# Transposes of a bank queued and issued one by one behind wide products, and the first activation sums of the MLP one piece later

## The chip, the cores and the metric

The kernel runs on one core of a Trainium2 chip. Time is device microseconds of one launch. TensorE (PE in the profile, with its weight loads as PEld) does matrix products and transposes, VectorE (DVE) and ScalarE (ACT) elementwise work, GpSimd (POOL) small work and some DMAs, SyncE (SP) issues most DMAs. Each engine works through its own list of instructions in order; semaphores hold an instruction until what it needs is there.

## The reference, cut to what matters

Two layers on 256 tokens of width 2048: an attention mixer (MLA) with an MLP, then a Mamba-2 mixer (SSM) with an MLP. Every mixer and MLP reads a normalised residual stream and adds to it.

```python
def squared_relu_mlp(h, w_in, w_out):          # 2048 -> 8192 -> 2048
    u = jax.nn.relu(h @ w_in)
    return (u * u) @ w_out

def reference(...):
    for i in range(DEPTH):                     # DEPTH = 2
        h = rms_norm(x, mix_norm_g[i])
        mix = mla_mixer(h, ...) if i % 2 == 0 else ssm_mixer(h, ...)
        x = x + mix
        h = rms_norm(x, mlp_norm_g[i])
        x = x + squared_relu_mlp(h, mlp_w_in[i], mlp_w_out[i])
    return x
```

The result must have float32 quality, and nearly all of the time goes into products of activations and weights.

## The kernel before, in words

**Products in halves.** Weights come from memory in pieces of 128 x 1024 floats (a "unit", tile `raw` or `rx`). ScalarE copies each to a rounded high half `wh` (line 102), VectorE subtracts that from the original to get the low half `wl` (line 103). [...] Activations are held in the same way, as a high and a low tile. A product is then three matrix products into one PSUM bank: high x high, low x high, high x low. These are the **wide products**, 128 x 128 weights of TensorE (an activation tile) against 512 columns: lines 339, 340 and 343 in `block`, and 616, 617 and 618 in `products` inside the MLP. 9216 of them, with 192 of 384 columns, fill most of TensorE's list. A unit of the MLP gives 6 or 12 of them.

**Transposes.** A product wants its activations with the contracted dimension on the partitions, so each result (128 tokens x 512 columns) is transposed before it can be used. `transposed` (line 316) takes a PSUM bank, issues four 128 x 128 transposes into its four quarters, and hands the bank to `split_out` (line 298): ScalarE copies it to the high tile (299), VectorE subtracts to the low tile (300). A transpose is a product with the identity `ident`, in one of two forms: as float32 (line 324), or as float32r words (line 322), for which GpSimd has first copied the source by DMA into a tile `tr`. A bank has three words and a float one, four of words, or four floats. The bank comes from the pools `sm` and `yp`, two banks each, or `sm` alone.

**Who calls it.** `finalize` at the ends of mixers and of the first MLP (both token tiles of one quarter of the width), `latent` in the MLA (queries `cq`, compressed keys and values `ckv`), `z_block` in the SSM, and `hidden` in the MLP, for each of the 32 activation blocks of an MLP. They are called with a delay: `later(n, fn)` runs `fn` n + 1 ticks on, and a tick follows each group of products; in the MLP, `turn` puts them in a list `due` with a time in microseconds, and `move` advances that clock by 1.36 or 2.72 per unit and runs what is due. The four transposes of a bank (or eight, where two calls are due together) thus stand in one row between two units.

**The order of the lists.** TensorE's list is in the order in which the code is written (`manual_schedule`). The lists of the other engines are ordered by a scheduler, by its own idea of when operands will be ready; so moving transposes also moves instructions on VectorE and ScalarE.

**The MLP's start.** The MLP forms sums of quarters of the weights and of the activations, so that seven products do the work of eight. The sums of weights are VectorE's line 183 (a weight tile plus another, both loaded by SyncE's DMAs at line 85). The sums of activations are `steps` from `combinations`: `one` (two whole tiles and more by line 528, a difference by line 538, a split to `sN`), `two` (more of these) and `three`. The first MLP product blocks need no sums (pieces `c`, eight units of 2.72 us by the clock in `move`); during them the sums are run, `when(5, steps[0])` and `when(10, steps[1])`: at the first piece whose end reaches 5 and 10 us, so behind the second and the fourth.

**Buffers.** Raw weights have 6 buffers, `wh` and `wl` 4 each. A load waits on SyncE until VectorE has read the tile that held its buffer.

Of the kernel before, what the change touches and what calls it, by code (L numbers as in the profile page):

```python
# [28 lines left out]
P = 128  # L29
# [29 lines left out]
class Unit:  # L59
# [3 lines left out]
    def __init__(self, key, nk, n, loads, make):  # L63
        self.key, self.nk, self.n, self.loads, self.make = key, nk, n, loads, make
# [150 lines left out]
class Trunk:  # L215
    def __init__(self, tc, ctx, d, out):
        self.tc, self.nc, self.d, self.out = tc, tc.nc, d, out
        nc = self.nc
        pool = lambda name, bufs, **kw: ctx.enter_context(tc.tile_pool(name=name, bufs=bufs, **kw))
        self.c = pool("const", 1)  # L220
        self.st = pool("stat", 24)
        self.res = pool("res", 1)
        self.xtp = pool("xt", 8)
        self.k4 = pool("k4", 8)
        self.s2 = pool("s2", 7)
        self.gb = pool("gb", 2)
        self.wp = {"raw": pool("raw", 6), "wh": pool("wh", 4), "wl": pool("wl", 4)}
        self.acc = pool("acc", 4, space=PSUM)
        self.sm = pool("sm", 2, space=PSUM)
        self.yp = pool("yp", 2, space=PSUM)  # L230
        self.queue, self.pump = [], None
        self.nsm = 0
        self.uid = 0

# [19 lines left out]
    def drain(self):  # L254
        while self.queue:
            self.tick()

    def stat(self, n):
        return self.st.tile([P, 16], F32, tag="st", name=self.name("st"))[:, :n]
# [54 lines left out]
        self.transposed(src, h[:, :, sl], lo[:, :, sl], wide)  # L314

    def transposed(self, src, h, lo, wide=True):
        b = self.bank(wide)
        src, words, n = src if isinstance(src, tuple) else (src, None, 0)
        for j in range(4):
            v = slice(j * P, (j + 1) * P)  # L320
            if j < n:
                self.nc.tensor.transpose(b.bitcast(F32R)[:, v], words[:, v], self.ident_r)  # L322
            else:
                self.nc.tensor.transpose(b[:, v], src[:, v], self.ident)  # L324
        self.split_out(h, lo, b.rearrange("p (k n) -> p k n", k=4))


    def block(self, keys, lhs, n=512, accs=None, first=True, last=True, mid=None):
        nc = self.nc
        if accs is None:  # L330
            accs = [self.acc_tile() for _ in range(2)]
        kt = 0
        for ik, key in enumerate(keys):
            for nk, wh, wl, end in self.flow.piece(key):
                en = last and ik == len(keys) - 1 and end
                for q in range(nk):
                    for t in range(2):
                        ah, al = lhs(kt + q, t)
                        nc.tensor.matmul(accs[t][:, :n], ah, wh[:, q, :], start=first and kt + q == 0, stop=False)  # L339
                        nc.tensor.matmul(accs[t][:, :n], al, wh[:, q, :], start=False, stop=False)  # L340
                for q in range(nk):
                    for t in range(2):
                        nc.tensor.matmul(accs[t][:, :n], lhs(kt + q, t)[0], wl[:, q, :], start=False, stop=en and q == nk - 1)  # L343
                kt += nk
                if mid and not end:
                    mid()
            self.tick()
        return accs
# [210 lines left out]
    def mlp_body(self, mp, layer, gain):  # L559
# [25 lines left out]
        S, steps = self.combinations(mp, xa)  # L585
        S["M1"], S["N4"], S["M2"] = xa[0, 0], xa[1, 1], xa[1, 0]
        out, bank, v, count = {}, {}, {}, {}
# [3 lines left out]
        def when(us, fn):  # L591
            due.append((at[0] + us, fn))
# [16 lines left out]
        def products(accs, key, lhs, kt, first, last):  # L609
            u, (h, lo) = self.flow.next(key)  # L610
            for q in range(2):
                k = 2 * kt + q
                wh, wl = h[:, q * 512:(q + 1) * 512], lo[:, q * 512:(q + 1) * 512]
                for t, b in enumerate(accs):
                    ah, al = lhs(k, t)
                    nc.tensor.matmul(b, ah, wh, start=first and q == 0, stop=False)  # L616
                    nc.tensor.matmul(b, ah, wl, start=False, stop=False)  # L617
                    nc.tensor.matmul(b, al, wh, start=False, stop=last and q == 1)  # L618

        sub = lambda o, a, b: nc.vector.tensor_tensor(o, a, b, ALU.subtract)  # L620
        plus = lambda o, a, b: nc.vector.tensor_tensor(o, a, b, ALU.add)
# [29 lines left out]

        tokens = plan()
        inside = False
        when(5, steps[0])
        when(10, steps[1])
        for tok in tokens:
            key = (tok[0], layer) + tok[1:]
            if tok[0] == "s":
                _, p, name, d = tok
# [3 lines left out]
                if count.setdefault(name, 0) % 4 == 0:  # L663
                    pool = self.sm if name == "N7" else self.acc
                    bank[name] = pool.tile([P, 512], F32, tag=pool.name, name=self.name("st"))
                count[name] += 1
                products([bank[name]], key, lambda k, t: [x[:, k] for x in S[name]], d,
                         count[name] % 4 == 1, count[name] % 4 == 0)
                if count[name] % 4 == 0:
                    after(name, p)  # L670
                move(1.36)
            elif tok[0] == "c":
                _, p, j, o = tok
                if o == 0:
                    out["c"] = pair_of_banks(self.yp if j else self.acc)
                products(out["c"], key, lhs_x, o, o == 0, o == 7)
                if o == 7:
                    for t in range(2):
                        turn(relu(out["c"][t], t), p, j, t, TR[4])
                    if j:  # L680
                        when(3, steps[2])
                if o % 2:
                    self.tick()
                move(2.72)
            else:
                _, p, nb, o = tok
                if o == 0:
                    out[nb] = pair_of_banks(self.yp)
                products(out[nb], key, lhs_u(p), o, o == 0, o == 3)
                if o == 3:  # L690
                    self.add_residual(nb, out.pop(nb))
                move(2.72)
# [915 lines left out]
```

## Time and profile before

| what | value |
|---|---|
| runs | 2287.46 us median of 3 (2285.67 to 2288.2) |
| profiled execution, first to last instruction | 2284.5 us |
| transposes of line 322 (words) | 229 into `sm`, 20 into `yp` |
| transposes of line 324 (floats) | 167 into `sm`, 16 into `yp` |
| weight splits, lines 102 and 103 | 986 each |
| loads of `wraw` and `wrx` from the page's DMA list | 512 KB each, 4.0 to 7.8 us to landing |

How to read the views that follow. A timeline row has the start in us, the length in us, engine, line, operation, out<-in, shape and count; rows of the same kind that follow each other are merged. A group row has busy us and the mean of one instruction in ns, then idle time before it. TensorE's products overlap, so their lengths say little; from one start to the next is what one costs. A weight load (PEld) begins as a rule when the product ahead of it starts.

### The profile page before, as it was taken

How to read it: one execution, taken by the hardware profiler on the slowest of the kernel's cores; microseconds unless marked ns; L12 is line 12 of the kernel's file. 1: busy time of each engine (PE TensorE's matmuls, PEld its weight loads, DVE VectorE, ACT ScalarE, POOL GpSimd, SP SyncE). 2: the span in 40 equal slices, each digit the busy share in tenths (PEclk: the TensorE clock that was granted, in tenths of full speed). 3: DMA queues.
4: the chain of work that ended last, by engine and by line, in shares of the span. 5: the costliest groups of instructions: out<-in, count | busy, mean ns of one | idle time of the engine just before them, and what ended most of it. 6: DMA issues, size and time to landing. Idle time of an engine off the chain costs nothing.

```text
span 2284.5 us, 30768 instructions
## 1 busy us (share of the span) xinstructions
PE 2278.1 (100%) x10929; PEld 1889.6 (83%) x10929; DVE 1915.9 (84%) x2318; ACT 1390.1 (61%) x1947; POOL 275.5 (12%) x315
## 2 busy tenths in 40 slices
PE   9999999999999999999999999999999999999999
PEld 7898888888888888888888888888888888888887
DVE  7786698999898897687899688676989889989985
ACT  7775576566666666564666555545666666666663
POOL 1440000000000000100133213121000000000000
PEclk9999999999999999999999999999999999999999
DMA  8545678888888878667888787767688888888874
GB/s 315 173 153 159 211 230 267 259 255 270 264 255 259 267 232 271 227 208 241 277 280 278 245 275 264 229 222 229 204 265 248 259 270 253 260 275 247 267 232 160
DMA packets 167706, 557.16 MB, mean 244 GB/s; under 512 B 19040, under 2 KB 28192, under 8 KB 166528
## 3 DMA queue, kind: packets, MB, share of 16 engines
q1 hardware_dynamic: 151264, 502.44, 66.2%
q0 software_dynamic: 13888, 48.49, 10.0%
q10 hardware_dynamic: 2400, 4.27, 0.5%
q8 instruction: 86, 1.41, 0.3%
q14 instruction: 68, 0.56, 0.1%
HBM read 529.65 MB, written 6.41 MB: 235 GB/s over the span
## 4 chain that ended last, share of the span: by engine, by line
PE 96%; DVE 1%; DMA 1%; ACT 1%; issue 1%; POOL 0%; SPq 0%; ACTq 0%; DVEq 0%
PE acc L339 13%; PE acc L340 13%; PE acc L343 13%; PE yp L618 9%; PE yp L617 9%; PE yp L616 9%; PE st L617 7%; PE st L618 7%; PE st L616 7%; DMA wraw<-mi 1%; PE sm L324 1%; DVE wl L103 1%; PE y L1309 1%; PE sm L322 1%; PE acc L616 1%; PE acc L618 1%
## 5 line engine op out<-in xcount | busy, mean ns | idle before, releaser
L102 ACT ACTIVATE wh<-wraw 128x1024 fp32r<-128x1024 f32 (+1 forms) x818 | 856.2, 1053 | 570.4 <-PE acc L340 268.9
L103 DVE TENSOR_TENSOR wl<-wraw,wh 128x1024 fp32r<-128x1024 f32 (+1 forms) x818 | 985.5, 1221 | 240.6 <-ACT wh L102 216.6
L616 PE MATMUL yp<-wh,k 128*128 128x512 f32 x896 | 349.2, 390 | 0.0
L618 PE MATMUL yp<-wh,k 128*128 128x512 f32 x896 | 348.8, 389 | 0.0
L617 PE MATMUL yp<-wl,k 128*128 128x512 f32 x896 | 348.6, 389 | 0.0
L339 PE MATMUL acc<-wh,xt 128*128 128x512 f32 x704 | 279.7, 397 | 0.4 <-ACT wh L102 0.4
L340 PE MATMUL acc<-wh,xt 128*128 128x512 f32 x704 | 274.9, 390 | 0.1
L102 ACT ACTIVATE wh<-wrx 128x1024 fp32r<-128x1024 f32 x168 | 177.8, 1058 | 153.4 <-PE yp L618 101.7
L103 DVE TENSOR_TENSOR wl<-wrx,wh 128x1024 fp32r<-128x1024 f32 x168 | 204.3, 1221 | 36.6 <-ACT wh L102 35.6
L618 PEld LDWEIGHTS yp<-wh,k 128*128 128x128 f32 x896 | 168.2, 188 | 35.1
L617 PEld LDWEIGHTS yp<-wl,k 128*128 128x128 f32 x896 | 168.2, 188 | 34.9
L616 PEld LDWEIGHTS yp<-wh,k 128*128 128x128 f32 x896 | 168.2, 188 | 34.8
L339 PE MATMUL acc<-wh,k 128*128 128x512 f32 x496 | 196.5, 396 | 0.0
L340 PE MATMUL acc<-wh,k 128*128 128x512 f32 x496 | 193.3, 390 | 0.0
L343 PE MATMUL acc<-wl,xt 128*128 128x512 f32 x704 | 188.3, 389 | 0.0
L616 PE MATMUL st<-wh,xt 128*128 128x512 f32 x448 | 177.7, 397 | 0.0
L618 PE MATMUL st<-wh,xt 128*128 128x512 f32 x448 | 174.9, 390 | 0.0
L617 PE MATMUL st<-wl,xt 128*128 128x512 f32 x448 | 174.7, 390 | 0.0
L339 PEld LDWEIGHTS acc<-wh,xt 128*128 128x128 f32 x704 | 132.7, 188 | 29.4 <-ACT wh L102 1.6
L340 PEld LDWEIGHTS acc<-wh,xt 128*128 128x128 f32 x704 | 132.5, 188 | 28.5 <-issue 1.2
L343 PEld LDWEIGHTS acc<-wl,xt 128*128 128x128 f32 x704 | 132.1, 188 | 27.7
L199 POOL DMA_DIRECT2D wrx<-mi x56 | 49.2, 878 | 720.6 <-DVE wl L103 524.5
(318 smaller groups left out, 3527.0 us busy)
## 6 DMA issues: line engine op xcount, KB each, us to landing
wraw<-mi SPq DMA_DIRECT2D x256, 512.0 KB, 5.5
wraw<-mo SPq DMA_DIRECT2D x256, 512.0 KB, 5.6
wraw<-si SPq DMA_DIRECT2D x160, 512.0 KB, 5.2
wraw<-so SPq DMA_DIRECT2D x64, 512.0 KB, 5.2
wrx<-mi SPq DMA_DIRECT2D x56, 512.0 KB, 5.4
wrx<-mi POOLq DMA_DIRECT2D x56, 512.0 KB, 7.8
wraw<-wo SPq DMA_DIRECT2D x32, 512.0 KB, 4.0
taps<-xD SPq DMA_DIRECT2D x16, 768.0 KB, 8.4
```

The source lines that it names most:

```text
L102: self.last = nc.scalar.activation(h[:, v], raw[:, v], AF.Copy)
L103: self.last_lo = nc.vector.tensor_tensor(lo[:, v], raw[:, v], h[:, v].bitcast(F32), ALU.subtract)
L199: nc.gpsimd.dma_start(st["b11"].tile, quarter(d, 1, 0), accum_op=ALU.add)
L322: self.nc.tensor.transpose(b.bitcast(F32R)[:, v], words[:, v], self.ident_r)
L324: self.nc.tensor.transpose(b[:, v], src[:, v], self.ident)
L339: nc.tensor.matmul(accs[t][:, :n], ah, wh[:, q, :], start=first and kt + q == 0, stop=False)
L340: nc.tensor.matmul(accs[t][:, :n], al, wh[:, q, :], start=False, stop=False)
L343: nc.tensor.matmul(accs[t][:, :n], lhs(kt + q, t)[0], wl[:, q, :], start=False, stop=en and q == nk - 1)
L616: nc.tensor.matmul(b, ah, wh, start=first and q == 0, stop=False)
L617: nc.tensor.matmul(b, ah, wl, start=False, stop=False)
L618: nc.tensor.matmul(b, al, wh, start=False, stop=last and q == 1)
L1309: nc.tensor.matmul(y[t][c, o], part(t)[:, c], xg[g][t][:, o], start=True, stop=True)
```

## The change

`transposed` no longer issues its four transposes. It puts four functions in a list `drops`; each, when called, issues one transpose (the first also takes the bank, the fourth also issues `split_out`). `drip` runs the first function of the list. Behind every wide product, `block` and `products` call `drip` once. `flush` empties the list at the very end. In the MLP the times of `one` and `two` go from 5 and 10 to 8 and 12, so they run behind the third and the fifth piece.

```diff
+        self.drops = []
...
+    def drip(self):
+        if self.drops:
+            self.drops.pop(0)()
+
+    def flush(self):
+        while self.drops:
+            self.drip()
...
     def transposed(self, src, h, lo, wide=True):
-        b = self.bank(wide)
         src, words, n = src if isinstance(src, tuple) else (src, None, 0)
-        for j in range(4):
-            v = slice(j * P, (j + 1) * P)
+        bank = []
+
+        def one(j):
+            if not bank:
+                bank.append(self.bank(wide))
+            b, v = bank[0], slice(j * P, (j + 1) * P)
             if j < n:
                 self.nc.tensor.transpose(b.bitcast(F32R)[:, v], words[:, v], self.ident_r)
             else:
                 self.nc.tensor.transpose(b[:, v], src[:, v], self.ident)
-        self.split_out(h, lo, b.rearrange("p (k n) -> p k n", k=4))
+            if j == 3:
+                self.split_out(h, lo, b.rearrange("p (k n) -> p k n", k=4))
+
+        for j in range(4):
+            self.drops.append(lambda j=j: one(j))
...
                         nc.tensor.matmul(accs[t][:, :n], ah, wh[:, q, :], start=first and kt + q == 0, stop=False)
+                        self.drip()
                         nc.tensor.matmul(accs[t][:, :n], al, wh[:, q, :], start=False, stop=False)
+                        self.drip()
...
                         nc.tensor.matmul(accs[t][:, :n], lhs(kt + q, t)[0], wl[:, q, :], start=False, stop=en and q == nk - 1)
+                        self.drip()
...
                     nc.tensor.matmul(b, ah, wh, start=first and q == 0, stop=False)
+                    self.drip()
                     nc.tensor.matmul(b, ah, wl, start=False, stop=False)
+                    self.drip()
                     nc.tensor.matmul(b, al, wh, start=False, stop=last and q == 1)
+                    self.drip()
...
-        when(5, steps[0])
-        when(10, steps[1])
+        when(8, steps[0])
+        when(12, steps[1])
```

In TensorE's list the transposes before stand in 48 rows of three word transposes and a float one, 16 rows of four float ones, 15 rows of seven and one, and 7 rows of eight float ones: 249 and 183. After, each of the 432 has a wide product ahead of it and one behind it. In the lists below the number behind a tile's name is its place in the program, and the lines of the changed kernel are its own (322 and 324 are 335 and 337 there, 616 to 618 are 636, 638 and 640).

TensorE, first MLP: the transposes of one block of hidden activations, from the words `tr_3785`. Before, as one row between two units:

```order
L617 MATMUL yp_3896<-wl_3867,k_432_3270 128x512
L618 MATMUL yp_3896<-wh_3866,k_433_3271 128x512
L322 MATMUL sm_3933<-ident,tr_3785 128x128 x3
L324 MATMUL sm_3933<-ident,s_457_3776 128x128
L616 MATMUL yp_3895<-wh_3878,k_445_3557 128x512
L617 MATMUL yp_3895<-wl_3879,k_445_3557 128x512
L618 MATMUL yp_3895<-wh_3878,k_446_3558 128x512
```

and after:

```order
L640 MATMUL yp_3896<-wh_3866,k_433_3271 128x512
L636 MATMUL yp_3895<-wh_3878,k_445_3557 128x512
L335 MATMUL sm_3940<-ident,tr_3785 128x128
L638 MATMUL yp_3895<-wl_3879,k_445_3557 128x512
L335 MATMUL sm_3940<-ident,tr_3785 128x128
L640 MATMUL yp_3895<-wh_3878,k_446_3558 128x512
L335 MATMUL sm_3940<-ident,tr_3785 128x128
L636 MATMUL yp_3896<-wh_3878,k_445_3557 128x512
L337 MATMUL sm_3940<-ident,s_457_3776 128x128
L638 MATMUL yp_3896<-wl_3879,k_445_3557 128x512
```

The bank is complete four wide products later than before, and the same number of instructions stands in the list.

VectorE at the start of the first MLP, from the whole activation tiles (line 528, 548 after) to the split of the first unit of the second column of `c` pieces (`wl_3214`). Before:

```order
L528 TENSOR_TENSOR xf_3190<-xt_2881,xt_2882 128x1024
L528 TENSOR_TENSOR xf_3137<-xt_2883,xt_2884 128x1024
L103 TENSOR_TENSOR wl_3165<-wraw_3144,wh_3164 128x1024
L538 TENSOR_TENSOR xf_3137<-xf_3133,xf_3137 128x1024
L103 TENSOR_TENSOR wl_3196<-wraw_3162,wh_3195 128x1024
L538 TENSOR_TENSOR xf_3133<-xf_3133,xf_3135 128x1024
L300 TENSOR_TENSOR sN_425_3141<-xf_3137,sN_424_3140 128x1024
L538 TENSOR_TENSOR xf_3135<-xf_3135,xf_3137 128x1024
L300 TENSOR_TENSOR sN_427_3182<-xf_3133,sN_426_3181 128x1024
L538 TENSOR_TENSOR xf_3190<-xf_3190,xf_3135 128x1024
L300 TENSOR_TENSOR sN_429_3187<-xf_3135,sN_428_3186 128x1024
L103 TENSOR_TENSOR wl_3214<-wraw_3193,wh_3213 128x1024
```

and after:

```order
L548 TENSOR_TENSOR xf_3155<-xt_2883,xt_2884 128x1024
L183 TENSOR_TENSOR wraw_3249<-wraw_3247,wraw_3249 128x1024
L558 TENSOR_TENSOR xf_3155<-xf_3151,xf_3155 128x1024
L103 TENSOR_TENSOR wl_3183<-wraw_3162,wh_3182 128x1024
L558 TENSOR_TENSOR xf_3151<-xf_3151,xf_3153 128x1024
L310 TENSOR_TENSOR sN_425_3159<-xf_3155,sN_424_3158 128x1024
L558 TENSOR_TENSOR xf_3153<-xf_3153,xf_3155 128x1024
L310 TENSOR_TENSOR sN_427_3200<-xf_3151,sN_426_3199 128x1024
L558 TENSOR_TENSOR xf_3208<-xf_3208,xf_3153 128x1024
L310 TENSOR_TENSOR sN_429_3205<-xf_3153,sN_428_3204 128x1024
L103 TENSOR_TENSOR wl_3214<-wraw_3180,wh_3213 128x1024
```

The sum of two weight tiles (183, `wraw_3249`), which stood three rows behind `wl_3214` before, now stands nine rows ahead of it. The second MLP has the same two orders.

VectorE in the MLA, from the split of a unit (`wl_799`, after `wl_785`) to the next but one; `ckv` is the compressed keys and values, and the queries `qn` (line 887, 910 after) are made in between. Before (two more rows like the last two follow):

```order
L103 TENSOR_TENSOR wl_799<-wraw_726,wh_798 128x768
L300 TENSOR_TENSOR ckv_202<-sm_782,ckv_201 128x4x128
L300 TENSOR_TENSOR ckv_202<-sm_789,ckv_201 128x4x128
L887 SCALAR_TENSOR_TENSOR qn_840<-acc_724,st_824,cst 128x128
L887 SCALAR_TENSOR_TENSOR qn_840<-acc_724,st_824,cst 128x64
L887 SCALAR_TENSOR_TENSOR qn_840<-acc_725,st_824,cst 128x128
L887 SCALAR_TENSOR_TENSOR qn_840<-acc_725,st_824,cst 128x64
```

and after:

```order
L103 TENSOR_TENSOR wl_785<-wraw_726,wh_784 128x768
L910 SCALAR_TENSOR_TENSOR qn_840<-acc_724,st_824,cst 128x128
L910 SCALAR_TENSOR_TENSOR qn_840<-acc_724,st_824,cst 128x64
L910 SCALAR_TENSOR_TENSOR qn_840<-acc_725,st_824,cst 128x128
L310 TENSOR_TENSOR ckv_202<-sm_789,ckv_201 128x4x128
L910 SCALAR_TENSOR_TENSOR qn_840<-acc_725,st_824,cst 128x64
L910 SCALAR_TENSOR_TENSOR qn_840<-acc_725,st_824,cst 128x128
L910 SCALAR_TENSOR_TENSOR qn_840<-acc_725,st_824,cst 128x64
L103 TENSOR_TENSOR wl_869<-wraw_744,wh_868 128x768
L310 TENSOR_TENSOR ckv_202<-sm_800,ckv_201 128x4x128
```

The two splits of `ckv` stood ahead of the last six `qn`; now the first stands behind three of them and the second behind all six and a weight split. In TensorE's list 12 products stood between the last transpose of `ckv` and its first reader, now 4.

More of the change, by code (lines that the diff above doesn't have):

```diff
@@ L256, in drain @@
             self.tick()
+        self.flush()
+    def drip(self):
[4 more added lines that the diff above has]
+            self.drip()
     def stat(self, n):
```

## The prediction

> **What bounds the kernel now.** I read the page first (busy times, the chain that ended last), then TensorE's timeline at a quiet place.
>
> ```profile
> span 2284.5 us, 30768 instructions
> PE 2278.1 (100%) x10929; PEld 1889.6 (83%) x10929; DVE 1915.9 (84%) x2318; ACT 1390.1 (61%) x1947; POOL 275.5 (12%) x315
> PE 96%; DVE 1%; DMA 1%; ACT 1%; issue 1%; POOL 0%; SPq 0%; ACTq 0%; DVEq 0%
> ...
> 859.69 0.39 PE L616 MATMUL st<-wh,xt 128*128 128x512 f32 x1
> ...
> 871.93 0.39 PE L616 MATMUL st<-wh,xt 128*128 128x512 f32 x1
> ```
>
> TensorE is never idle, and 96% of the chain is its own. Durations overlap (a wide product shows 0.39 us), so what an instruction costs is read from start to start: 54 wide products begin between 859.69 and 871.93, 12.24 / 54 = 0.227 us each. Whatever makes TensorE's list longer by a microsecond makes the kernel longer by one. VectorE at 84% has little room and becomes the second term.
>
> **The price of a transpose in a row today.** The timeline of TensorE at one row of each kind:
>
> ```profile
> 374.82 0.37 PE L322 MATMUL sm<-ident,tr 128*128 128x128 f32 x3
> 375.02 0.30 PE L324 MATMUL sm<-ident,s 128*128 128x128 f32 x1
> 375.08 0.48 PE L616 MATMUL yp<-wh,k 128*128 128x512 f32 x1
> 375.39 0.40 PE L617 MATMUL yp<-wl,k 128*128 128x512 f32 x1
> ...
> 377.93 0.39 PE L616 MATMUL st<-wh,xt 128*128 128x512 f32 x1
> ...
> 232.14 0.46 PE L322 MATMUL yp<-ident,tr 128*128 128x128 f32 x4
> ...
> 233.05 0.39 PE L340 MATMUL acc<-wh,k 128*128 128x512 f32 x1
> ...
> 298.08 0.60 PE L324 MATMUL sm<-ident,s 128*128 128x128 f32 x4
> ...
> 298.75 0.40 PE L617 MATMUL yp<-wl,xt 128*128 128x512 f32 x1
> ```
>
> A row is measured from its first transpose to the second wide product behind it, less one wide product. Three word transposes (L322) and a float one (L324): 375.39 - 374.82 - 0.227 = 0.343 us. Seven and one: 233.05 - 232.14 - 0.227 = 0.683. Four float ones: 298.75 - 298.08 - 0.227 = 0.443. The order of instructions has 48, 15 and 16 such rows, and 7 rows of eight float ones, which I take as two of four, 0.886. Together 16.5 + 10.2 + 7.1 + 6.2 = **40.0 us** for 249 word and 183 float transposes. Behind a row a tail follows: the 11 wide products from 375.39 to 377.93 take 2.54 instead of 2.49, so 0.05 us per row. I take one tail per bank as unchanged.
>
> **The price of a lone one.** No transpose stands alone in the trace of before, so it is bounded by neighbours. First the means of the groups, weight loads ahead:
>
> ```profile
> L618 PEld LDWEIGHTS yp<-wh,k 128*128 128x128 f32 x896 | 168.2, 188 | 35.1
> L322 PEld LDWEIGHTS sm<-ident,tr 128*128 128x128 f32 x229 | 26.0, 139 | 7.5
> L366 PEld LDWEIGHTS sm<-cst,s 128*128 128x128 f32 x8 | 1.1, 192 | 0.0
> L322 PE MATMUL sm<-ident,tr 128*128 128x128 f32 x229 | 26.9, 236 | 0.0
> L324 PE MATMUL yp<-ident,s 128*128 128x128 f32 x16 | 2.4, 272 | 0.0
> ...
> 981.12 0.56 PE L366 MATMUL sm<-cst,s 128*128 128x64 f32 x4
> ...
> 981.80 0.40 PE L340 MATMUL acc<-wh,xt 128*128 128x512 f32 x1
> ```
>
> Four float transposes span 0.60 us (298.08) and one lasts 0.272, so they start (0.60 - 0.272) / 3 = 0.109 apart, which is about what 128 columns of them stream. Three word transposes span 0.37 us, so they start (0.37 - 0.236) / 2 = 0.067 apart. Now what must be loaded next. A transpose's own load lasts 139 ns, a wide product's 188: the load behind a lone transpose is always the long one. It begins when the instruction ahead of it starts, so 0.227 us of a wide product hide it, and 0.11 of a float transpose nearly do. A word transpose with 0.067 may not. The nearest row is L366: half as many float columns, so half of 0.11, about 0.055 us of stream, with a long load (192 ns) behind each. Four of them and the change to the wide products take 981.80 - 981.12 - 0.227 = 0.453, **0.113 each**, twice their stream. That is the value I take for a lone word transpose. For a lone float one I take the row of four less three intervals: 0.443 - 0.328 = **0.115**. After: 249 x 0.113 + 183 x 0.115 = 28.1 + 21.0 = 49.1 us, **+9.1** against 40.0. Today's rows are cheaper because a short load follows a short load.
>
> Bounds of the word price: 0.067 if the long load is hidden after all (-11.5 us, +9.1 becomes -2.4). Above, the load may not overlap at all: a wide product whose weights came late lost 0.11 (295.45 to 295.79 below is 0.34, not 0.227), so 0.067 + 0.11 = 0.18 (+16.7, 25.8). I stay at 0.113, which is the row nearest in kind, a short stream with a long load.
>
> The Trainium skill, page "TensorE: Matmul & The Clock Gate", section "Back-to-back issue gap", gives about 81 ns per product in a stream of loads and products of 128 columns; by it a lone word transpose would cost 0.081 and this term would be 20.2 + 21.0 - 40.0 = +1.2. No row here has such a transpose between wide products; L366's 0.113 speaks against it.
>
> **The banks are handed over later.** A bank's last transpose now ends four wide products later, and the second bank of a pair eight later (0.9 and 1.8 us). I cost this at nothing where the readers stand 16 to 38 wide products behind (3.6 us and more), which cover ScalarE's and VectorE's splits of 0.6 and 0.7 us; with that cover gone it costs the missing part, once per bank. The PSUM bank itself is held 0.9 us longer; in the MLPs the next one is asked for 4 us later, so nothing waits for it. SyncE's list keeps its order but for four swaps of neighbours, GpSimd's but for a few of its small ones. VectorE's and ScalarE's lists change more, and at two places (shown with the change) a wait comes of it.
>
> Start of an MLP:
>
> ```profile
> 279.36 1.23 DVE L103 TENSOR_TENSOR wl<-wraw,wh 128x1024 fp32r<-128x1024 f32 x1 [1.49 <-ACT wh L102]
> ...
> 281.69 2.35 DVE L528 TENSOR_TENSOR xf<-xt,xt 128x1024 f32<-128x1024 f32 x2
> 283.96 1.22 DVE L103 TENSOR_TENSOR wl<-wraw,wh 128x1024 fp32r<-128x1024 f32 x1
> ...
> 294.18 2.35 DVE L103 TENSOR_TENSOR wl<-wraw,wh 128x1024 fp32r<-128x1024 f32 x2
> ...
> 295.45 0.50 PE L617 MATMUL yp<-wl,xt 128*128 128x512 f32 x1
> 295.79 0.40 PE L618 MATMUL yp<-wh,xt 128*128 128x512 f32 x1
> ...
> 280.61 0.33 SPq L85 DMA_DIRECT2D wraw<-mi  x1
> ...
> DMA to landing us min/median/max: 6.5/6.5/6.5
> ```
>
> From 279.36 to 294.18 VectorE has no gap, one instruction of 1024 columns every 1.14 us, and the weight half that ends this stretch (294.18) reaches TensorE just late: 0.34 at 295.45 instead of 0.227. In the new order the sum of two weight tiles (L183) stands ahead of the activation sums, at about 285.2. Its second tile is fetched by SyncE's DMA of 280.61, which can't leave earlier: it needs the buffer that the L103 of 279.36 frees. It lands 6.5 us later, at 287.1. VectorE waits 1.9, and behind it stand L183 itself and eight more (three differences, three splits, one L103, one more difference): 9 x 1.14 = 10.3, so the weight half starts at 297.4, **3.2** later. TensorE comes there 0.1 later than now. What is late next is only what follows it in the same list, so this is paid once: +3.1. In the second MLP:
>
> ```profile
> 1614.98 0.33 SPq L85 DMA_DIRECT2D wraw<-mi  x1
> ...
> DMA to landing us min/median/max: 5.2/5.2/5.2
> ...
> 1628.56 2.35 DVE L103 TENSOR_TENSOR wl<-wraw,wh 128x1024 fp32r<-128x1024 f32 x2
> ```
>
> 1614.98 + 5.2 + 10.3 = 1630.5 against 1628.56: +1.9. Together **+5.0**, bounds 0 (VectorE makes it up) and 6.
>
> Compressed keys and values (ckv), where only four products separate the last transpose from its reader:
>
> ```profile
> 62.40 1.03 PE L324 MATMUL sm<-ident,s 128*128 128x128 f32 x8
> ...
> 66.41 0.50 PE L340 MATMUL acc<-wh,ckv 128*128 128x512 f32 x1
> ...
> 65.07 1.28 DVE L300 TENSOR_TENSOR ckv<-sm,ckv 128x512 fp32r<-128x512 f32 x2
> 66.27 1.44 DVE L887 SCALAR_TENSOR_TENSOR qn<-acc,st,cst 128x128 f32<-128x128 f32 x6
> 67.62 0.96 DVE L103 TENSOR_TENSOR wl<-wraw,wh 128x768 fp32r<-128x768 f32 x1
> ```
>
> Today both splits stand ahead of the six L887, and TensorE's 66.41 follows their end. After, the second split stands behind all six and an L103: 65.07 + 1.44 + 0.64 + 0.9 + 0.64 = 68.7, **+2.3** (bounds 0 and 3). The transposes themselves are ready by then: eight pairs of 0.173 + 0.115 from 62.40 end at 64.7.
>
> **Sum.** 9.1 + 5.0 + 2.3 = 16.4 us on the profiled 2284.5, so 2300.9. The median of the runs, 2287.46, stands 2.96 above that span, and I carry this over: **2304**.
>
> **Rivals.**
> 1. The stalls don't come, or a lone word transpose costs near what it costs in a row (0.343 / 4 = 0.086). For: VectorE's 84% leaves room somewhere. Against: each of the two engines works its list in order. The first gives 2287.5 + 9.1 = 2296.6; the second 21.4 + 21.0 - 40.0 + 7.3 = +9.7, 2297.
> 2. Slower still: the long load does not overlap with the short stream, 0.18. For: the 0.11 lost at 295.45. Against: L366. It gives 25.8 + 7.3 = +33, 2320; halfway 2312.
> 3. The other side, one mechanism: TensorE takes the long load in while the wide product ahead of the transpose still streams, so that a lone one costs its stream alone (0.067 and 0.109) and leaves no tail (86 tails of 0.05 are 4.3): 16.7 + 19.9 - 40.0 - 4.3 = -7.7, so 2280 without the stalls and 2287 with them. It decides below (40.0 + 4.3 - 4.6 - 19.9) / 249 = 0.08 us per word transpose. For: the wide products' own loads hide fully. Against: L366's 0.113, where nothing but loads could have set the pace. The Trainium skill, same page, section "The mechanism", says that TensorE pulls a weight load for its background buffer ahead of running products. By that rule this rival holds if the buffer is free, and in this row it evidently wasn't.
> 4. That nothing changes can be left out: in the new order every one of the 432 transposes has a wide product on both sides.
>
> **How the numbers follow.** Forecast 0.51 (2299 to 2309); rival 1 0.20; rival 2 0.12; rival 3 with the stalls 0.11, without them 0.06. A difference under 0.2% (4.6 us) can't be told from none by a measurement of this kernel. Above 2292.0 lie the forecast, rivals 1 and 2 and a little of 3: 0.84. Within: 0.10. Below 2282.9: 0.06. The range 2290 to 2315 holds the forecast, rival 1, half of rival 2 and the upper end of 3, about 0.82; it is wide because the word price has the bounds 0.067 and 0.18.
>
> **What would show it.** From one wide product to the second behind a lone word transpose, less two wide products: 0.113 says right, 0.067 rival 3, 0.18 rival 2. For a float one 0.115. VectorE idle ahead of the first L183 of each MLP until a DMA landed, and TensorE waiting some 3 and 2 us at the first product with the second column's low halves; a wait of about 2 us more at ckv. Were the transposes cheap and the kernel still slower, the stalls would carry it; were there no stalls, 2297 would be seen.

## The result and the profile after

| what | before | after |
|---|---|---|
| runs, median | 2286.82 us (4 runs) | 2304.8 us (2301.84, 2302.05, 2307.55, 2307.62) |
| ratio of the runs | | 1.008, 95% interval 1.0066 to 1.0094 |
| profiled execution, first to last instruction | 2284.5 us | 2299.9 us (+15.4) |

The changed kernel is slower by 0.8%. Its runs stand in two pairs, and the median lies between them; the profiled execution is of the faster pair. First the page of the changed kernel: span, busy times, and the shares of the chain that ended last.

```profile
span 2299.9 us, 30769 instructions
PE 2287.3 (99%) x10929; PEld 1890.2 (82%) x10929; DVE 1919.8 (83%) x2318; ACT 1394.9 (61%) x1947; POOL 272.1 (12%) x315
PE 98%; DVE 1%; DMA 1%; issue 0%; ACT 0%; SPq 0%; DVEq 0%
```

The number of instructions on the two engines is the same as before, and TensorE still carries the chain. So the 15.4 us are TensorE's list made longer, by dearer instructions or by waits inside it. Next TensorE's timeline after, at the transposes of one hidden block (three words, L335, and a float, L337), and at a bank of four floats.

```profile
378.51 0.39 PE L636 MATMUL yp<-wh,k 128*128 128x512 f32 x1
378.74 0.22 PE L335 MATMUL sm<-ident,tr 128*128 128x128 f32 x1
378.80 0.45 PE L638 MATMUL yp<-wl,k 128*128 128x512 f32 x1
379.09 0.22 PE L335 MATMUL sm<-ident,tr 128*128 128x128 f32 x1
379.15 0.45 PE L640 MATMUL yp<-wh,k 128*128 128x512 f32 x1
379.44 0.22 PE L335 MATMUL sm<-ident,tr 128*128 128x128 f32 x1
379.50 0.45 PE L636 MATMUL yp<-wh,k 128*128 128x512 f32 x1
...
301.97 0.48 PE L638 MATMUL yp<-wl,xt 128*128 128x512 f32 x1
302.29 0.27 PE L337 MATMUL sm<-ident,s 128*128 128x128 f32 x1
302.32 0.49 PE L640 MATMUL yp<-wh,xt 128*128 128x512 f32 x1
302.64 0.27 PE L337 MATMUL sm<-ident,s 128*128 128x128 f32 x1
302.67 0.48 PE L636 MATMUL yp<-wh,xt 128*128 128x512 f32 x1
```

From one wide product to the next with a transpose between them are 0.35 us in both places. Less the 0.227 of a wide product, a lone transpose costs **0.12 us, word or float**. Added up over all 432 from the starts in the two traces (with the slow wide products behind a bank, the tails), transposes take 43.0 us before and 52.3 after: **+9.3**.

The weight loads of the same place:

```profile
378.75 0.19 PEld L638 LDWEIGHTS yp<-wl,k 128*128 128x128 f32 x1
378.88 0.15 PEld L335 LDWEIGHTS sm<-ident,tr 128*128 128x128 f32 x1
379.09 0.19 PEld L640 LDWEIGHTS yp<-wh,k 128*128 128x128 f32 x1
```

The load of the wide product (L638) starts at 378.75, with the transpose ahead of it (378.74), not earlier. That is so throughout: of the 10929 loads of this trace the median one starts 0.003 us after the product ahead of its own, and none more than 0.05 us before it. So only that short stream can hide it. (The row of the load, 0.19 us, reaches past the start of its product's own row, 378.80, so the 0.19 isn't the price.)

Then the waits of TensorE after (us in total, times, longest):

```profile
PE yp L638 <- DVE wl L103: 4.9, 2, 2.6
PE acc L358 <- DVE ckv L310: 2.1, 2, 1.4
```

The two waits of the first row are at the two MLP starts. VectorE's timeline there:

```profile
285.54 1.22 DVE L548 TENSOR_TENSOR xf<-xt,xt 128x1024 f32<-128x1024 f32 x1
287.57 1.22 DVE L183 TENSOR_TENSOR wraw<-wraw,wraw 128x1024 f32<-128x1024 f32 x1 [0.82 <-DMA wraw<-mi]
...
297.80 2.35 DVE L103 TENSOR_TENSOR wl<-wraw,wh 128x1024 fp32r<-128x1024 f32 x2
...
1630.72 1.23 DVE L183 TENSOR_TENSOR wraw<-wraw,wraw 128x1024 f32<-128x1024 f32 x1 [1.41 <-DMA wraw<-mi]
```

and TensorE's:

```profile
296.37 0.39 PE L636 MATMUL yp<-wh,xt 128*128 128x512 f32 x1
299.07 0.50 PE L638 MATMUL yp<-wl,xt 128*128 128x512 f32 x1 [2.31 <-DVE wl L103]
...
1639.20 0.39 PE L636 MATMUL yp<-wh,xt 128*128 128x512 f32 x1
1642.21 0.50 PE L638 MATMUL yp<-wl,xt 128*128 128x512 f32 x1 [2.62 <-DVE wl L103]
...
1643.33 0.63 PE L640 MATMUL yp<-wh,xt 128*128 128x512 f32 x1
1643.76 0.63 PE L636 MATMUL yp<-wh,xt 128*128 128x512 f32 x1
...
1645.89 0.63 PE L640 MATMUL yp<-wh,xt 128*128 128x512 f32 x1
```

At each MLP start VectorE stands at the weight sum (L183) until its DMA landed, the weight half starts at 297.80, and TensorE waits: 299.07 - 296.37 - 0.227 = 2.47 and 1642.21 - 1639.20 - 0.227 = 2.78 us; before TensorE didn't wait there. (The 0.11 and 0.07 us that it lost just behind these places before, it loses here too: 299.07 is followed at 299.40.) So **+5.25**. Behind the second wait seven wide products start 0.427 apart instead of 0.227: **+1.4**, which the prediction doesn't have.

The wide products, and all else that isn't a transpose of a bank, are the same 10497 instructions in the same order in both kernels. So the lag of the k-th of them behind its twin can be followed through the run:

| place, in the time of before | added lag, us |
|---|---|
| start to 61.5 | -0.2 |
| 61.5 to 68, ckv | +2.2 |
| 68 to 118, attention | -1.5 |
| 118 to 279 | -0.3 |
| 279 to 303, start of the first MLP | +3.1 |
| 303 to 1628, first MLP, SSM | +6.3 |
| 1628 to 1646, start of the second MLP | +4.4 |
| 1646 to the end | +1.4 |

At ckv the two waits of the row with L310 came (TensorE's timeline after):

```profile
66.34 0.50 PE L358 MATMUL acc<-wh,ckv 128*128 128x512 f32 x1 [0.72 <-DVE ckv L310]
68.45 0.50 PE L358 MATMUL acc<-wh,ckv 128*128 128x512 f32 x1 [1.37 <-DVE ckv L310]
```

Behind them most of it is given back. Before, TensorE waited twice in the attention part, which the changed kernel, being late, no longer does. TensorE's timeline of before:

```profile
71.88 0.63 PE L939 MATMUL yp<-ident,qn 128*128 128x128 f32 x4 [0.41 <-DVE qn L887]
...
107.08 0.44 PE L939 MATMUL yp<-ident,kn 128*128 128x128 f32 x2 [0.55 <-ACT xt L944]
```

### The profile page after: what moved, and what is told of

It reads as the page before. It is cut to its first block, busy times and chain, and to the rows that moved or that the text cites. A ratio compares the mean times of both kernels' runs of the same rounds, so it can differ in the third digit from the quotient of the medians.

```text
span 2299.9 us, 30769 instructions
## 1 busy us (share of the span) xinstructions
PE 2287.3 (99%) x10929; PEld 1890.2 (82%) x10929; DVE 1919.8 (83%) x2318; ACT 1394.9 (61%) x1947; POOL 272.1 (12%) x315
## 4 chain that ended last, share of the span: by engine, by line
PE 98%; DVE 1%; DMA 1%; issue 0%; ACT 0%; SPq 0%; DVEq 0%
PE acc L356 13%; PE acc L358 13%; PE acc L362 13%; PE yp L638 10%; PE yp L640 10%; PE yp L636 9%; PE st L638 8%; PE st L636 8%; PE st L640 8%; PE sm L337 1%; PE y L1332 1%; PE sm L335 1%; PE acc L748 0%; PE acc L640 0%; PE acc L638 0%; PE acc L636 0%
## 5 line engine op out<-in xcount | busy, mean ns | idle before, releaser
L638 PE MATMUL yp<-wl,k 128*128 128x512 f32 x896 | 349.8, 390 | 0.0
L638 PEld LDWEIGHTS yp<-wl,k 128*128 128x128 f32 x896 | 168.2, 188 | 35.8 <-DVE wl L103 0.3
L638 PE MATMUL st<-wl,xt 128*128 128x512 f32 x448 | 179.6, 401 | 0.0
```

## The experiments

My theory had three separate parts: a lone transpose shows the weight load behind it (+9.3), two waits at the MLP starts come of VectorE's order, and one at ckv too. The rivals: the loss comes from the later hand-over of banks, from the later activation sums, from the float form, or from a VectorE so full that its waits only move. Each time is a median; before took 2286.0 to 2286.4 in the four groups of runs.

**1. The two values.** The changed kernel again, unaltered.

> The changed kernel once more, since its four runs stood in two pairs, 2302 and 2307.6 us. My theory: the two waits of TensorE at the MLP starts (2.6 and 2.9 us in the profiled run) lie near a length after which the granted clock falls for some microseconds; in the profiled run it fell behind the second wait only, and in the runs of 2307.6 behind a further one or for longer. Then both values appear again, and a profile of the longer kind has a second stretch of wide products at 0.43 us each of some 5 us. Rival: the pairs are scatter between chips or calls; then the runs here agree within 0.3%, around one value.

2303.74, 2304.86, 2306.32 and 2307.41 us: a spread of 0.16%, not two values, so that point of mine fell. The profiled execution has a span of 2305.5. The mean granted clock in three stretches, each with a wait, first after, then this run. A row has the stretch and its length in us, the busy time of PE, PEld, DVE, ACT and POOL, then PEclk, the granted clock as a share of the full one, and two columns on the DMAs:

```profile
66.00:72.00 6.00, 4.29 (x18) 3.24 (x19) 3.08 (x9) 2.25 (x9) 4.12 (x6) 1.00 0.57 173
298.00:307.00 9.00, 7.93 (x38) 6.40 (x38) 9.00 (x9) 5.01 (x7) 0.00 (x0) 1.00 0.75 248
1642.00:1652.00 10.00, 9.79 (x40) 7.73 (x40) 8.71 (x9) 4.45 (x6) 0.00 (x0) 0.83 0.72 224
```

```profile
66.00:72.00 6.00, 4.51 (x12) 3.25 (x13) 3.09 (x11) 2.03 (x8) 4.10 (x6) 0.72 0.51 169
298.00:307.00 9.00, 5.48 (x15) 4.21 (x14) 8.07 (x8) 4.59 (x8) 0.00 (x0) 0.64 0.84 287
1642.00:1652.00 10.00, 7.75 (x28) 5.88 (x27) 10.00 (x10) 6.26 (x9) 0.00 (x0) 0.84 0.80 257
```

The clock fell behind all three waits here, behind one only in the other profile. So the scatter between executions of one kernel is, in the main, how many of its waits are followed by half clock. The eight runs of the changed kernel bear this out: with a mean granted clock of 0.999 they took 2301.8 to 2303.7 us, with 0.998 2304.9 to 2306.3, and with 0.997 2307.4 to 2307.6. (The wait of the first MLP was 3.68 here instead of 2.47, because the DMA landed later.)

**2. The later sums alone**, with rows as before.

```diff
-        when(5, steps[0])
-        when(10, steps[1])
+        when(8, steps[0])
+        when(12, steps[1])
```

> The kernel before with the second part of the change alone: activation sums at 8 and 12 instead of 5 and 10, transposes in rows. VectorE's list keeps the first weight sum behind the activation sums. Theory (the waits at the MLP starts come from the late transposes of the residual stream, which move the sum of weights ahead in VectorE's list): no wait of 2 us or more at the MLP starts, 2286.8 +- 2 us. Rival (the later activation sums alone delay the first unit of the second column): two waits as in the changed kernel, +5 us, 2292.

2286.35 us, ratio 0.9999 (0.9990 to 1.0008), no wait at the MLP starts. That part of the change costs nothing.

**3. Rows in the same place, and pairs.** A drip issues a whole bank, or two transposes.

```diff
-        for j in range(4):
-            self.drops.append(lambda j=j: one(j))
+        self.drops.append(lambda: [one(j) for j in range(4)])
```

```diff
-        for j in range(4):
-            self.drops.append(lambda j=j: one(j))
+        for j in (0, 2):
+            self.drops.append(lambda j=j: [one(j), one(j + 1)])
```

> The changed kernel, but the first drip of a bank issues its four transposes in a row. The weight sum stands behind the activation sums again. Theory (price of lone transposes +9.5 us, waits at MLP starts +5.2 with 1.5 of half clock): transposes back at about 43 us, no MLP-start wait, -16: about 2288 us (2286 to 2291). Rival (the later hand-over of the banks, and not the single transposes, carries the loss): 2295 or more.

> The changed kernel, but a drip issues two transposes. The weight sum stands behind the activation sums again. Theory (each stretch of transposes pays once, about 0.05 us, for the long weight load at its end, beside some 0.08 us per word and 0.10 per float transpose): a bank of three words and a float goes from 0.50 to 0.44, 108 banks -6 us; with the MLP-start waits gone 2304.8 - 6 - 6.7 = about 2292. Rival (every transpose near a wide product costs its full lone price): 0.50 per bank stays, 2298.

Rows: 2286.97 us, ratio 1.0004 (0.9995 to 1.0013). The queue and the place behind a wide product cost nothing; the loss comes of issuing singly, directly and by the order on VectorE that follows from it. Pairs: 2289.58, ratio 1.0014 (1.0005 to 1.0023), lower than my 2292, as the waits at ckv went too (0.3 us left of 2.1). Transposes take 46.5 us there. A bank of three words and a float costs 0.39 us in a row, 0.43 in pairs and 0.50 singly, some 0.035 more for each further stretch; four floats cost 0.49, 0.50 and 0.50.

**4. Floats only.**

```diff
-            if j < n:
+            if j < 0:
```

> All 432 transposes in the float32 form, the word copies by GpSimd still made but not read. Theory (a lone transpose costs the long weight load behind it, whatever it streams): a former word transpose goes from about 0.121 to the 0.115 of the float ones, 249 x -0.006 = -1.5 us, so 2301 to 2306 us, no more than the changed kernel. Rival (a lone transpose costs its own stream plus a fixed part): float streams 0.109 against 0.067, 249 x 0.042 = +10.5 us, 2315.

2325.15 us, 20 more than the changed kernel: both expectations fell by their time. But transposes take 53.0 us there against 52.3, as the theory said. The rest are TensorE's waits on VectorE: 20.4 us for low halves against 4.9 in the changed kernel, one of 1.3 at an activation split (L310), and three stretches of half clock instead of one. VectorE itself waits at weight sums. The group of the first weight sums, before, after and here, busy us and mean ns, then idle time and what ended it:

```profile
L183 DVE TENSOR_TENSOR wraw<-wraw,wraw 128x1024 f32<-128x1024 f32 x56 | 68.4, 1222 | 18.3 <-DMA wraw<-mi 18.1
```

```profile
L183 DVE TENSOR_TENSOR wraw<-wraw,wraw 128x1024 f32<-128x1024 f32 x56 | 68.4, 1221 | 18.0 <-DMA wraw<-mi 17.9
```

```profile
L183 DVE TENSOR_TENSOR wraw<-wraw,wraw 128x1024 f32<-128x1024 f32 x56 | 68.4, 1222 | 41.7 <-DMA wraw<-mi 41.5
```

One of these waits in the timeline of this run, on VectorE:

```profile
479.69 1.23 DVE L183 TENSOR_TENSOR wraw<-wraw,wraw 128x1024 f32<-128x1024 f32 x1 [1.77 <-DMA wraw<-mi]
480.83 2.35 DVE L103 TENSOR_TENSOR wl<-wraw,wh 128x1024 fp32r<-128x1024 f32 x2
```

and on TensorE:

```profile
482.10 0.50 PE L638 MATMUL yp<-wl,k 128*128 128x512 f32 x1 [1.51 <-DVE wl L103]
```

The scheduler had set more of these sums ahead of a weight split, as at the MLP starts. The second of the three group rows is instructive: the idle time of the group is the same before and after. What changed there is which instructions stood behind the waiting one.

**5. The boundary's banks in rows**, all others singly.

```diff
-  self.later(int(early), lambda ...: self.transposed(xg, h, lo, wide))
+  self.later(int(early), lambda ...: (self.transposed(xg, h, lo, wide), self.flush()))
```

> The changed kernel, but the transposes of finalize (the residual stream at the ends of mixers and of the first MLP) go in rows as before. VectorE's first weight sum of an MLP stands behind the activation sums again. Theory: both waits at the MLP starts go (2.6 and 2.9 us, less 0.2 that were there before), and with them the 8 products at half clock (1.5 us) and the second value near 2307.6; 28 banks in rows instead of singly give another 28 x 0.1 = 2.8 us. Profiled span 2299.9 - 5.3 - 1.5 - 2.8 = about 2290, runs 2292 to 2293, all within 1.5 us. Rival (the waits only move to the next place of the same VectorE list, which is nearly full): -2.8 alone, 2299 to 2302.

2294.89 us (2292.89 to 2296.16, so 2 above what I had), span 2291.0: 8.9 below the profiled 2299.9, where I had 9.6. No wait at either MLP start, no half clock. The waits come of the late transposes of the residual stream, and didn't move elsewhere.

**6. Only the order on VectorE repaired**, first for every opening sum of weights, with word and float transposes and on the kernel before.

```diff
-                add("b22", "b12", "b22")
+                with flow.tc.issue_after(flow.last_lo.ins):
+                    add("b22", "b12", "b22")
```

> The changed kernel with all its lone transposes and TensorE's list unaltered; only on VectorE the sum of weights that opens a group of the MLP (the first of line 183) is held behind the weight split that was written ahead of it. Theory (two separate costs, lone transposes +9.5 and waits): the waits at both MLP starts go (2.47 and 2.78 in the profile of the changed kernel) with the half clock of 1.5, the one at ckv (1.5) stays: span 2299.9 - 6.8 = 2293, runs 2294 to 2297. Transposes stay at 52 us in the sum by banks. Rival (VectorE is so full that the wait only moves to a later unit): 2300 or more.

> All transposes as floats, as in the run of floats alone that took 2325 us, with the same sum of weights held back. Theory (in that run 23 us of the excess were waits of VectorE at sums of weights set ahead of a weight split, and a lone float transpose costs no more than a lone word one, 0.5 us over all): the time comes within 2 us of the run with words and the same hold. Rival (float transposes are themselves dearer, 0.042 to 0.08 each on 249): 10 to 20 us above it.

> The kernel before with nothing but the sum of weights held back on VectorE. In its profile TensorE waits 0.94 us in all at four first products of the MLP groups (at 570, 737, 1821 and 1905 us). Theory: these go, -0.9 us, 2285.4, at the edge of what can be measured. Rival (the held sums are late themselves, a unit of the group waits for them): 2287 to 2295.

2312.11, 2312.97 and 2297.93 us. As a repair it was a miss: on the kernel before the hold alone costs 11.7 us. TensorE waits there 4.6 us for low halves and 2.4 for high ones, against four small waits of 0.9 together before; that the held sums come late themselves is my reading of it. The MLP-start waits did shrink (0.55 us at the first, 0.27 at the second), but the profile of the first of the three shows others:

```profile
PE st L640 <- DVE wl L103: 5.0, 10, 1.2
```

It settles the float question all the same: with the promoted sums gone, floats cost 0.9 us more than words, not 20. Had a lone transpose cost its own stream and a fixed part, it would have been 10.5.

**7. The first sum of each MLP only**, then with the transposes of cq and ckv in rows too.

```diff
+                with flow.tc.issue_after(flow.last_lo.ins) if layer not in flow.held else nullcontext():
+                    add("b22", "b12", "b22")
+                flow.held.add(layer)
```

> As the run that held every opening sum of weights, but only the first such sum of each MLP is held behind the weight split written ahead of it; TensorE's list is that of the changed kernel, and VectorE's differs only near the two MLP starts. Theory (the new waits of that run came from the other held sums, the lone transposes and the MLP-start waits are separate costs): waits at both MLP starts 0.6 us or less instead of 2.5 to 3.7 and 2.4 to 2.8, no half clock behind them, the wait at ckv (1.5) stays: profiled span 2299.9 - 4.5 - 1.5 = about 2294, runs 2294 to 2298; the 9.5 us of the transposes stay. Rival (VectorE has no room for the activation sums and the held weight sum together, whatever their order): 2300 or more.

> The same, and the transposes of latent in rows as before, so all three waits are repaired and 416 of... all but the 8 banks of cq and ckv are transposed singly. Theory: another -1.5 (ckv wait) and -0.8 (8 banks in rows): 2292 to 2295 us, which leaves the single transposes alone, +8.7 us less what the kernel before loses at its own small waits (0.9): 6 to 9 us above before. Rival (the waits only hid part of the transposes' cost or the other way round, so that the two do not add): outside 2290 to 2297.

2297.17 and 2295.7 us: the first as the theory had it, the second 0.7 above its range. TensorE's list in the first is that of the changed kernel to the instruction, so some 8 us of its loss were VectorE's order and the half clock behind it. (Its profiled execution, its slowest, has a span of 2297.2 where I had 2294; the wait at ckv was followed by half clock there.) Its first MLP start:

```profile
297.89 0.39 PE L639 MATMUL yp<-wh,xt 128*128 128x512 f32 x1
298.69 0.50 PE L641 MATMUL yp<-wl,xt 128*128 128x512 f32 x1 [0.40 <-DVE wl L103]
```

0.57 us instead of 2.47. In the second kernel, against before, three small waits of 0.3 us are new and four of 0.2 to 0.3 are gone, which nearly cancel. Its span is 2294.0: the single transposes alone, all but the 8 banks of cq and ckv, are **+9.5 us**, ratio 1.0041 (1.0028 to 1.0055).

**8. ckv alone in rows.**

```diff
-  fns.append(lambda ...: self.transposes(cn, tiles[0], tiles[1], t, wide))
+  fns.append(lambda ...: (self.transposes(cn, tiles[0], tiles[1], t, wide), self.flush()))
```

> The changed kernel, but the transposes of latent (queries cq, compressed keys and values ckv) go in rows as before. Theory: the wait of TensorE at the first product with ckv goes from 1.8 to about 0.3 us, -1.5, and 8 banks in rows give 8 x 0.1 = 0.8: -2.3 us against the changed kernel, whose two values stay. Rival (VectorE's place at ckv is late for another reason): -0.8 only.

2302.79 us against 2305.59, inside the scatter that half clock makes, so the time decides nothing. The lag does: from 61.5 to 118 it is 0.0 instead of 2.2 - 1.5 = +0.7. The wait at ckv goes, but what it cost was 0.7, in an execution without half clock behind it.

No version beats the kernel before; rows with the later sums stand level with it.

## Why the prediction was right, point by point

- **Transposes, +9.1.** Measured +9.3, and +9.5 with all else repaired. Within it two errors cancel. A lone word transpose is 0.12 instead of 0.113, a float one 0.12 instead of 0.115, so without the tails the step is +10.9. The tails, which I had left unchanged, shrank by some 1.6 us. The reading behind it held: a long load behind a short stream. Where the stream is 0.067 (words) the load shows, where it is 0.109 (floats) it nearly doesn't, and both end at the same price. Issued singly, the word form loses what it gains in a row, and that is the whole term. The Trainium skill's 81 ns per product ("TensorE: Matmul & The Clock Gate", "Back-to-back issue gap") is near what a word transpose costs in a row of seven and a float one, (0.683 - 0.115) / 7 = 0.081, and not what a lone one costs: 0.12.
- **MLP starts, +5.0.** Measured +5.25, but 2.47 and 2.78 where I had 3.1 and 1.9: the DMA behind each L183 was issued and landed at other times than in the trace of before. I put the shift on the new order as a whole; the runs show that the late boundary transposes make it, and that the times 8 and 12 have no part in it.
- **The half clock, not forecast.** "What is late next is only what follows it in the same list, so this is paid once" failed: +1.4 in the profiled execution (seven products, 0.2 us more each), and +5.0 in the repeated one (25 products).
- **ckv, +2.3.** The wait came, +2.2. The step that failed is that it stays: TensorE's later waits in the attention part took up 1.5, because what they wait for didn't move with TensorE. "TensorE is never idle" had passed over these waits of before.
- **Small waits of before** at 570, 737, 1821 and 1905 us, 0.9 together, went, and I hadn't counted them.

Sum: 9.3 + 5.25 + 1.4 + 2.2 - 1.5 - 0.9 = 15.8 against the 15.4 measured, and 16.4 forecast. So the price of the transposes and the two waits of the MLPs were rightly foreseen, cause and size. That the sum came so near is partly luck: the three terms that I didn't have, +1.4, -1.5 and -0.9, nearly cancel. And that the median came within 1 us of 2304 is luck too: it lies among executions whose half clock differs by more than that. Rival 1 (2296.6, no waits) is what the second kernel of experiment 7 comes near to, with 2295.7. Rival 2 (0.18) and rival 3 (a load taken in early) fell with the 0.12 and with the load that starts at 378.75.

## What to carry to other kernels

A short matrix product between long ones shows the long weight load behind it, so put short ones in a row; spreading them among long ones hid nothing here, and a longer stream didn't help either (a lone float transpose costs the same 0.12 as a lone word). Before spreading work out, look at which instruction on another engine moves ahead with it: one that waits for a DMA in front of a busy list costs its wait to everybody behind it. And price a wait against the waits that come later, which may take it up, and with the chance of half clock behind it, which cost another 1.4 us in the profiled execution here.

## What was not expected of the hardware

After waits of TensorE of 1.5 to 3.7 us the granted clock was at half for a while (a wide product takes 0.427 instead of 0.227 us then), in some executions and not in others: the wait of 1.54 us at ckv was followed by it in 2 of 7 profiles that have that wait, one of 2.47 was not, one of 2.41 was. So the length alone doesn't decide.

The traces show what does. They record when the granted clock changes, and within each trace all changes lie whole multiples of 3.413 us apart. In the changed kernel there are 1638.4 us (480 of them) at full clock up to 1643.14, then one interval at half, then 655.4 us (192) at full clock. So the clock changes only at marks of a fixed grid, and what counts is how long TensorE stood idle between two marks. Four intervals of the changed kernel, columns as in experiment 1 (idle is the length less PE's busy time, the first number behind it):

```profile
294.85:298.26 3.41, 1.91 (x9) 1.25 (x7) 3.41 (x4) 3.38 (x6) 0.00 (x0) 1.00 0.76 221
298.26:301.67 3.41, 2.60 (x11) 2.17 (x12) 3.41 (x4) 1.53 (x3) 0.00 (x0) 1.00 0.90 286
1639.73:1643.14 3.41, 0.93 (x4) 0.80 (x5) 3.41 (x4) 3.18 (x5) 0.00 (x0) 1.00 0.94 265
1643.14:1646.55 3.41, 3.41 (x10) 2.62 (x9) 3.41 (x4) 0.00 (x0) 0.00 (x0) 0.50 0.86 311
```

A mark at 298.26 cuts the wait of the first MLP into 1.50 and 0.81 us, and the clock stays. The wait of the second MLP leaves 2.48 us idle between two marks, and the next interval is at half. Over all 14 profiles, TensorE at full clock stood idle for 1.73 us or more in 14 intervals, and half clock followed each of them; in all others it was 1.64 or less, and half clock followed none. An edge near half an interval fits them all (the ends of products are modelled, so it is known only roughly). Two intervals at half clock in which TensorE was idle for 0.88 and 1.07 us were followed by a second one at half. The grid lies elsewhere in each execution (its first mark on record is 4.3 to 7.5 us behind the first instruction), so whether a given wait is followed by half clock is partly chance.

The Trainium skill, same page, section "What's actually happening", says that the clock falls after an idle window of about 3.4 us, and that this window runs on by itself. The second is what these traces show; the first asks for more than they do, as 1.73 us of 3.41 were enough.
